# Three small moves in the token mixers: two parted products, V copies behind the first item, a granule chained later

## The chip, the cores and the metric

The kernel runs on one core of one Trainium2 chip. The metric is device time in microseconds, the median of the runs. A core has TensorE (PE in the profile, with its weight loads as PEld), VectorE (DVE), ScalarE (ACT), GpSimd (POOL) and SyncE (SP, which here only issues DMAs).

## The reference

A trunk of two layers on 512 tokens of width 1024, all in float32. A layer is a half-step SwiGLU FFN, a mixers' stage, and a second half-step FFN:

```python
x = x + 0.5 * swiglu(rms_norm(x, ffn1_norm[l]), ffn1_w_in[l], ffn1_w_out[l])
h = rms_norm(x, mix_norm[l]) @ w_mix_in[l]
(c_x, c_b, c_c, h_q, h_f, h_i, h_g, f_q, f_k, f_v, f_f) = jnp.split(h, split_at, axis=-1)
y = jnp.concatenate([
    short_conv_mixer(c_x, c_b, c_c, conv_w[l]),
    hgrn2_mixer(h_q, h_f, h_i, h_g, lower_bounds[l], hgrn_out_gain[l]),
    fox_mixer(f_q, f_k, f_v, f_f, fox_f_bias[l], fox_q_gain[l], fox_k_gain[l]),
], axis=-1)
x = x + y @ w_mix_out[l]
x = x + 0.5 * swiglu(rms_norm(x, ffn2_norm[l]), ffn2_w_in[l], ffn2_w_out[l])
```

The short convolution has 256 channels and three taps. HGRN2 is a gated linear recurrence with four heads of 64, done in chunks of 64 tokens. FoX is causal attention with eight heads of 64, normalised q and k, and a forget gate that adds the difference of cumulative log gates to the logits. D_FF is 2816.

## The kernel before

**Products in three.** Each float32 operand is parted into a high part (rounded to `fp32r`) and a low part, the rest. A product is then three TensorE products, high by high, high by low and low by high, in `mm3` (L322, L330, L331). With `parted=True` the first of the three, high by high, is issued as two halves over the moving operand's columns, so four instructions instead of three. The FFN asks for that at the first product of three of its blocks (`PARTED`, used in `halved`).

**Granules.** Weights come in granules: `granule` loads two rows of 128 (`kk` = 2, or the one that is left) into a buffer `st` (two of them) by SP, and `parted` makes the two parts in a buffer `hl` (three of them): the high part by ACT (L311), the low part by DVE (L312). With `ahead` true this runs at high priority and in one piece. With `ahead` false it has no priority, comes in `kk` pieces, and each piece is put into a given order behind the last named instruction of ACT and of DVE (`follow`, `self.chain`). `stream_steps` yields after each granule's products. Its argument `calm` makes the first granule (`k == 0`) one with `ahead` false.

**The order of instructions.** The kernel is written in Tile: each engine runs its own instructions in order, but what order that is, Tile's scheduler decides from the order in the code, priorities, and what it takes to be ready. The kernel's `NOSYNC` dependencies fix an order where it wants one.

**The mixers' stage** (`mix`) runs once in each layer. It first projects HGRN2's inputs. Then `hgrn`, a generator, alternates with `dense`, the projections of FoX (`fox_qkv`): at each yield `hgrn` says how many granules of `dense` follow, which are 1, 2, 4, 4, 4, 3, 2, 1, 0, 2. `hgrn` issues bursts of small products (64 rows by 64 columns of the array) for the transposes, states and scores of its chunks, and the dense granules fill the time in which DVE and ACT work on them. A granule of `dense` is 2 rows x 4 token tiles x 3 products of 256 columns, 24 in all.

`fox_qkv` runs for two halves of four heads (`hf` = 0, 1). For each it projects q, k and V, and copies V out of two PSUM banks, with the tokens' scale, as a high part (ACT, L1550) and a low part (DVE, L1551); token tiles 0 and 1 lie in the first bank, 2 and 3 in the second. For `hf` = 1 the second bank is `po`, of which there is only one. V of `hf` = 1 is first read in the second run of the attention.

The attention (`fox_attend`) works through 16 items in a run, a head and a tile of 128 queries each. An item has scores (L1602, L1603) issued three items ahead, a softmax (L1607, L274, L1611, L1613 or L1615), four transposes at most into a bank `pt` (L1666; two such banks), their copies PH (ACT, L1668) and PL (DVE, L1669), and, once for two items, the product with V (L1625) into the bank `po`. At a head's first item `fox_prep` also transposes q and k of the head after next into a `pt` bank (L1565), from which KA (ACT, L1570) and QA (DVE, L1571) are made.

`beside` interleaves the attention with dense work: the first run with the convolution's projections (`conv`), the second with five of the eight rows of the output projection (`most`). When `n` is 3 in the first run, `finish` issues HGRN2's end (L1481 to L1490). Last, the stage does the other three rows (`rows(5, ...)`) in two halves of 512 columns, `dg` = 0 and 1; the first of them is `calm`.

Of the kernel before, what the change touches and what calls it, by code (L numbers as in the profile page):

```python
# [1 line left out]

# [39 lines left out]

SKEW_HELD, SKEW_MOVING = 16, 48
PARTED = (10, 16)
EPS = 1e-6
CH = 64
NCH = T // CH
HD = 64
# [109 lines left out]
class Trunk:  # L158
# [8 lines left out]
    def __init__(self, ctx, tc):  # L167
        self.tc = tc
        self.nc = tc.nc
        nc = self.nc  # L170
        self.const = ctx.enter_context(tc.tile_pool(name="const", bufs=1))
        self.res = ctx.enter_context(tc.tile_pool(name="res", bufs=1))
        self.wp = ctx.enter_context(tc.tile_pool(name="wp", bufs=1))
        self.ps = ctx.enter_context(
            tc.tile_pool(name="ps", bufs=1, space=bass.MemoryType.PSUM)
        )
        self.ident = self.const.tile([P, P], F32, tag="ident", name="ident")
        make_identity(nc, self.ident)
        self.ones_mean = self.const.tile([P, P], F32R, tag="ones_mean", name="ones_mean")
        nc.vector.memset(self.ones_mean.bitcast(F32), 1.0 / D)  # L180
        self.epsc = self.const.tile([P, 1], F32, tag="epsc", name="epsc")
        nc.vector.memset(self.epsc, EPS)
        self.xT = self.res.tile([P, KD, T], F32, tag="xT", name="xT")

        self.xh, self.xl = [None] * KD, [None] * KD
        self.uid = 0
        self.ntog = 0
        self.tab, self.tab_users, self.loaded = None, [], None
        self.chain = {}
        self.entry, self.between = {}, {}  # L190
# [127 lines left out]
    def mm3(self, acc, ah, al, bh, bl, first, last, parted=False, keep=False, lows=False):  # L318
        nc = self.nc
        n = bh.shape[-1]  # L320
        for c in (slice(0, n // 2), slice(n // 2, n)) if parted else (slice(0, n),):
            i = nc.tensor.matmul(  # L322
                acc[:, c], ah, bh[:, c], start=first and c.start == 0, stop=False,
                skip_group_check=True,
            )
            if keep:
                self.follow("p", i)
        rest = [(ah, bl), (al, bh)]
        (a, b), (c, d) = rest[::-1] if lows else rest
        nc.tensor.matmul(acc, a, b, start=False, stop=False, skip_group_check=True)  # L330
        i = nc.tensor.matmul(acc, c, d, start=False, stop=last, skip_group_check=True)  # L331
        if keep:
            self.follow("p", i)
# [690 lines left out]
    def mix(self, l, w, w_out, conv_w, out_gain, q_gain, k_gain, f_bias, next_gain):  # L1024
# [3 lines left out]
        with tc.tile_pool(name=self.n("mix"), bufs=1) as mp:  # L1028
# [98 lines left out]
                zf, v[:, :, 256:264], fb.unsqueeze(1).to_broadcast([P, 4, NH])  # L1127
            )
            half = [{}, {}]

            def projections():
                for hf in range(2):
# [5 lines left out]
            for part, n in enumerate(hgrn):  # L1138
                if n is None:
                    break  # L1140
                if n == 0:
                    left.close()
                    ap1 = left.enter_context(
                        tc.tile_pool(name=self.n("at"), bufs=1, reuse_waits="tile")
                    )
                    for tag in ("PH", "PL"):
                        ap1.tile([P, 4, 2, P], F32R, tag=tag, name=self.n(tag), bufs=2)
                    self.qb = pair(ap1, "QB", F32R)
                    for t in self.qb:
                        nc.gpsimd.memset(t[64:66, :].bitcast(F32), 1.0)  # L1150
                    ops = {h: self.fox_prep(ap1, h, half[0][0], qkg, "sc") for h in range(2)}
                if part < 2:
                    next(decay, None)
                for _ in range(n):
                    next(dense, None)
            attend = self.fox_attend(ap1, 0, half, qkg, ops)
# [30 lines left out]
            def beside(attend, dense, first=0, then=()):  # L1187
                for _ in range(first):
                    next(dense, None)
                for n, _ in enumerate(attend, first):  # L1190
                    if n == 3 and then:
                        then()
                    if n >= 2:
                        next(dense, None)
                for _ in dense:
                    pass
# [4 lines left out]
            def rows(k0, a, n):  # L1201
                return lambda k, kk: [
                    w_out[order[k0 + k] * P : (order[k0 + k] + kk) * P, a : a + n]
                ]
# [19 lines left out]
            self.ntog = 0  # L1224
            for dg in range(2):
                banks = self.next4()
                self.stream(
                    [(bk, c, None) for bk, c in zip(banks, TOK)],
                    rows(5, 512 * dg, 512), act(5), 3, calm=dg == 0,
                )  # L1230
                for i in range(4):
                    j = 4 * dg + i
                    add(j, banks[i])
                    self.norm_part(j, ap2)
# [286 lines left out]
    def fox_qkv(self, mp, hf, tokens, half):  # L1521
        nc = self.nc
        qk = mp.tile([P, 4, 4, 2, HD], F32, tag="qk", name=self.n("qk"), bufs=2)
        for w, a in enumerate((F_Q, F_K)):
            banks = yield from tokens(a + 256 * hf, ("mm", "mm" if w == hf else "po"))
            s16 = lambda tag: mp.tile([P, 4, 4], F32, tag=tag, name=self.n(tag), bufs=2)
            m, r, t = s16("fm"), s16("fr"), s16("ft")
            bc = lambda c: c.unsqueeze(2).to_broadcast([P, 4, 4])
            two = lambda bi: slice(2 * bi, 2 * bi + 2)
            src = [x.rearrange("p (i h d) -> p i h d", i=2, h=4) for x in banks]  # L1530
            for bi in range(2):
                out = qk[:, two(bi), :, w, :]
                nc.scalar.activation(out, src[bi], AF.Square)
                nc.vector.reduce_sum(m[:, two(bi)], out, axis=AX.X)
            nc.vector.tensor_mul(m, m, bc(self.inv2))
            self.act(r, m, AF.Ln, bias=self.epsc)
            self.act(r, r, AF.Exp, scale=-0.5)
            self.rsqrt(r, m, r, t)
            nc.vector.tensor_mul(r, r, bc(self.invc))
            for bi in range(2):  # L1540
                out = qk[:, two(bi), :, w, :]
                nc.vector.tensor_mul(
                    out, src[bi], r[:, two(bi)].unsqueeze(3).to_broadcast([P, 2, 4, HD])
                )
        V = mp.tile([P, 4, 4, 2, HD], F32R, tag="V", name=self.n("V"), bufs=2)
        for bi, bank in enumerate((yield from tokens(F_V + 256 * hf, ("mm", "po" if hf else "mm")))):
            for i in (2 * bi, 2 * bi + 1):
                src = bank[:, 256 * (i % 2) : 256 * (i % 2) + 256].rearrange("p (h d) -> p h d", d=HD)
                sc = self.invc[:, i : i + 1]
                nc.scalar.activation(V[:, i, :, 0, :], src, AF.Copy, scale=sc)  # L1550
                nc.vector.scalar_tensor_tensor(  # L1551
                    out=V[:, i, :, 1, :], in0=src, scalar=sc, in1=V[:, i, :, 0, :],
                    op0=ALU.mult, op1=ALU.subtract,
                )
        half[hf] = qk, V

    def fox_prep(self, pool, h, qk, g, tag="pt", second=None):
# [35 lines left out]
    def fox_attend(self, pool, hf, half, g, ops):  # L1593
# [55 lines left out]
        for n, (h, i) in enumerate(items):  # L1649
            yield  # L1650
            if n + LOOK < len(items):
                h2, i2 = items[n + LOOK]
                pb[h2, i2] = scores(ops[h2], i2)
            if i == 0 and h + 2 < NH:
                ops[h + 2] = self.fox_prep(
                    pool, h + 2, half[(h + 2) // 4][0], g, second=nc.gpsimd
                )
            if i % 2 == 0:
                PH, PL = (
                    pool.tile([P, 4, 2, P], F32R, tag=t_, name=self.n(t_), bufs=2)  # L1660
                    for t_ in ("PH", "PL")
                )
            tb = self.bank("pt")
            p = pb.pop((h, i))
            for j in range(i + 1):
                nc.tensor.transpose(tb[:, j * P : (j + 1) * P], p[:, j * P : (j + 1) * P], self.ident)  # L1666
            t3 = tb.rearrange("p (j t) -> p j t", j=4)[:, : i + 1, :]
            nc.scalar.copy(PH[:, : i + 1, i % 2, :], t3)  # L1668
            nc.vector.tensor_sub(PL[:, : i + 1, i % 2, :], t3, PH[:, : i + 1, i % 2, :])  # L1669
            if len(late) and n >= late[0][0] + LAG:  # L1670
                values(*late.pop(0)[1:])
            if i % 2:
                late.append((n, h, i, PH, PL))
        for a in late:
            values(*a[1:])

# [211 lines left out]
```

## Time and profile before

| | us |
|---|---|
| median of three runs | 1805.09 |
| lowest and highest | 1804.33, 1806.71 |
| the profiled execution | 1806.13 |
| its span | 1804.4 |
| busy: PE, DVE, ACT, POOL | 1796.0, 1442.3, 992.8, 176.9 |

The span runs from the first to the last instruction of the program; the profiled execution's own time has some 1.7 us more around it. Matmul records overlap, since each one lasts to the modelled end of its pipeline: the pace of PE is read from one start to the next, not from the durations. The mixers' stage stands at about 340 to 575 us in the first layer and 1230 to 1465 in the second. A row of the timeline gives start, length, engine, line, operation, what is written and read, the shape, the count, and in brackets the idle time before it with what ended it. A row of the chain gives start, length, and what ran.

### The profile page before, as it was taken

How to read it: one execution, taken by the hardware profiler on the slowest of the kernel's cores; microseconds unless marked ns; L12 is line 12 of the kernel's file. 1: busy time of each engine (PE TensorE's matmuls, PEld its weight loads, DVE VectorE, ACT ScalarE, POOL GpSimd, SP SyncE). 2: the span in 40 equal slices, each digit the busy share in tenths (PEclk: the TensorE clock that was granted, in tenths of full speed). 3: DMA queues.
4: the chain of work that ended last, by engine and by line, in shares of the span. 5: the costliest groups of instructions: out<-in, count | busy, mean ns of one | idle time of the engine just before them, and what ended most of it. 6: DMA issues, size and time to landing. Idle time of an engine off the chain costs nothing.

```text
span 1804.4 us, 34742 instructions
## 1 busy us (share of the span) xinstructions
PE 1796.0 (100%) x14267; PEld 1683.9 (93%) x14267; DVE 1442.3 (80%) x2020; ACT 992.8 (55%) x1427; POOL 176.9 (10%) x184
## 2 busy tenths in 40 slices
PE   9999999999999999999999999999999999999999
PEld 7899999899888899999889999998998888999997
DVE  8889887676887898879679887876868778888893
ACT  5455555454776464556445555555547755555551
POOL 0011120100000001112001111201000000020210
PEclk9999999999999999999999999999999999999999
DMA  6658784333433767868266787923234346687762
GB/s 199 186 130 191 183 173 98 76 83 84 105 98 102 220 139 161 196 161 172 82 197 139 171 181 191 174 65 83 78 81 112 92 140 186 164 159 192 157 136 94
DMA packets 244638, 254.09 MB, mean 141 GB/s; under 512 B 18904, under 2 KB 228576, under 8 KB 244480
## 3 DMA queue, kind: packets, MB, share of 16 engines
q1 hardware_dynamic: 189424, 182.38, 33.7%
q0 software_dynamic: 54752, 69.23, 23.8%
q8 instruction: 112, 1.84, 0.4%
q14 instruction: 46, 0.38, 0.1%
q10 hardware_dynamic: 304, 0.27, 0.0%
HBM read 223.98 MB, written 2.10 MB: 125 GB/s over the span
## 4 chain that ended last, share of the span: by engine, by line
PE 93%; DVE 2%; ACT 2%; DMA 1%; issue 1%; SPq 0%; ACTq 0%; DVEq 0%
PE mm L322 13%; PE mm L331 13%; PE mm L330 13%; PE sc L330 6%; PE sc L322 6%; PE sc L331 6%; PE pt L322 6%; PE pt L330 6%; PE pt L331 6%; PE po L331 3%; PE po L322 3%; PE po L330 3%; PE po L1625 1%; PE pt L1666 1%; DMA st<-in_ffn_w_in_dram 1%
## 5 line engine op out<-in xcount | busy, mean ns | idle before, releaser
L804 ACT CAST hl<-w 128x1024 fp32r<-128x1024 f32 x322 | 336.8, 1050 | 310.7 <-PE mm L331 85.4
L806 DVE TENSOR_TENSOR hl<-w,hl 128x1024 fp32r<-128x1024 f32 x322 | 392.4, 1222 | 80.4 <-ACT hl L804 80.1
L312 DVE TENSOR_TENSOR hl<-st,hl 128x512 fp32r<-128x512 f32 (+3 forms) x194 | 162.5, 838 | 116.4 <-ACT hl L311 115.4
L311 ACT CAST hl<-st 128x512 fp32r<-128x512 f32 (+3 forms) x194 | 142.8, 737 | 171.7 <-PE po L331 64.6
L322 PE MATMUL mm<-xc,hl 128*128 128x256 f32 (+1 forms) x733 | 201.2, 276 | 0.0
L330 PE MATMUL mm<-xc,hl 128*128 128x256 f32 x728 | 201.2, 276 | 0.0
L331 PE MATMUL mm<-xc,hl 128*128 128x256 f32 x728 | 201.0, 276 | 0.0
L322 PE MATMUL sc<-xc,hl 128*128 128x256 f32 (+1 forms) x532 | 146.0, 276 | 0.0
L330 PE MATMUL sc<-xc,hl 128*128 128x256 f32 x528 | 146.0, 276 | 0.0
L331 PE MATMUL sc<-xc,hl 128*128 128x256 f32 x528 | 145.8, 276 | 0.0
L322 PEld LDWEIGHTS mm<-xc,hl 128*128 128x128 f32 x733 | 137.4, 188 | 0.2
L330 PEld LDWEIGHTS mm<-xc,hl 128*128 128x128 f32 x728 | 136.7, 188 | 0.0
L331 PEld LDWEIGHTS mm<-xc,hl 128*128 128x128 f32 x728 | 136.7, 188 | 0.0
L322 PE MATMUL pt<-xc,hl 128*128 128x256 f32 (+1 forms) x482 | 132.6, 276 | 0.0
L330 PE MATMUL pt<-xc,hl 128*128 128x256 f32 x480 | 132.6, 276 | 0.0
L331 PE MATMUL pt<-xc,hl 128*128 128x256 f32 x480 | 132.5, 276 | 0.0
L322 PE MATMUL mm<-x,hl 128*128 128x512 f32 x272 | 107.6, 396 | 0.0
L331 PE MATMUL mm<-x,hl 128*128 128x512 f32 x272 | 106.2, 390 | 0.0
L330 PE MATMUL mm<-x,hl 128*128 128x512 f32 x272 | 106.1, 390 | 0.0
L322 PEld LDWEIGHTS sc<-xc,hl 128*128 128x128 f32 x532 | 99.7, 188 | 0.2
L330 PEld LDWEIGHTS sc<-xc,hl 128*128 128x128 f32 x528 | 99.1, 188 | 0.0
L331 PEld LDWEIGHTS sc<-xc,hl 128*128 128x128 f32 x528 | 99.1, 188 | 0.0
(512 smaller groups left out, 5583.1 us busy)
## 6 DMA issues: line engine op xcount, KB each, us to landing
w<-in_ffn_w_in_dram SPq DMA_DIRECT2D x140, 512.0 KB, 5.5
w<-in_ffn_w_out_dram SPq DMA_DIRECT2D x64, 512.0 KB, 4.5
w<-in_ffn_w_out_dram POOLq DMA_DIRECT2D x56, 512.0 KB, 8.4
st<-in_w_mix_in_dram SPq DMA_DIRECT2D x88, 256.0 KB, 2.7
st<-in_ffn_w_in_dram SPq DMA_DIRECT2D x70, 256.0 KB, 3.2
w<-in_ffn_w_in_dram POOLq DMA_DIRECT2D x35, 512.0 KB, 8.1
w<-S POOLq DMA_DIRECT2D x35, 512.0 KB, 4.8
st<-in_ffn_w_out_dram SPq DMA_DIRECT2D x24, 512.0 KB, 5.5
```

What stands on the lines that cost most here:

```text
L311: a = nc.scalar.copy(hi, src[:, c : c + w])
L312: b = nc.vector.tensor_sub(lo, src[:, c : c + w], hi)
L322: i = nc.tensor.matmul(acc[:, c], ah, bh[:, c], start=first and c.start == 0, stop=False, skip_group_check=True,)
L330: nc.tensor.matmul(acc, a, b, start=False, stop=False, skip_group_check=True)
L331: i = nc.tensor.matmul(acc, c, d, start=False, stop=last, skip_group_check=True)
L804: A(nc.scalar.copy(hi, src))
L806: return lambda: V(nc.vector.tensor_sub(lo, src, hi))
L1625: nc.tensor.matmul(self.ob[:, t0 + u * P : t0 + 2 * P], V[:, j, h % 4].rearrange("p a d -> p (a d)"), part[:, j, u:, :].rearrange("p i t - ...
L1666: nc.tensor.transpose(tb[:, j * P : (j + 1) * P], p[:, j * P : (j + 1) * P], self.ident)
```

## The change

Three things, all in the mixers' stage.

- `PAIRS = (1, 5)`: after the yields 1 and 5 of `hgrn` (counted from 0) a counter `self.pair` is set to 2, and `mm3` parts the product at which it comes to 0. This is the second product of the next dense granule, twice in each layer.
- For `hf` = 1 the copies of V's second bank (token tiles 2 and 3) are put on a list, `self.later`, and issued in `beside` when `n` is 1, which is after the first item of the first attention run.
- The first granule of `dg` = 1 becomes `calm` as well, and before it the chain of ACT and DVE is set to `self.turned`: the copies PH and PL of the last head's item with `i == 2` in the second attention run.

```diff
+PAIRS = (1, 5)
...
     def mm3(self, acc, ah, al, bh, bl, first, last, parted=False, keep=False, lows=False):
         nc = self.nc
         n = bh.shape[-1]
+        if self.pair:
+            self.pair -= 1
+            parted |= self.pair == 0
         for c in (slice(0, n // 2), slice(n // 2, n)) if parted else (slice(0, n),):
...
                 if part < 2:
                     next(decay, None)
+                if part in PAIRS:
+                    self.pair = 2
                 for _ in range(n):
                     next(dense, None)
...
                 for n, _ in enumerate(attend, first):
+                    if n == 1:
+                        for copy in self.later:
+                            copy()
+                        self.later = []
                     if n == 3 and then:
                         then()
...
             for dg in range(2):
                 banks = self.next4()
+                if dg:
+                    self.chain["a"], self.chain["v"] = self.turned
                 self.stream(
                     [(bk, c, None) for bk, c in zip(banks, TOK)],
-                    rows(5, 512 * dg, 512), act(5), 3, calm=dg == 0,
+                    rows(5, 512 * dg, 512), act(5), 3, calm=True,
                 )
...
-        for bi, bank in enumerate((yield from tokens(F_V + 256 * hf, ("mm", "po" if hf else "mm")))):
-            for i in (2 * bi, 2 * bi + 1):
-                src = bank[:, 256 * (i % 2) : 256 * (i % 2) + 256].rearrange("p (h d) -> p h d", d=HD)
-                sc = self.invc[:, i : i + 1]
-                nc.scalar.activation(V[:, i, :, 0, :], src, AF.Copy, scale=sc)
-                nc.vector.scalar_tensor_tensor(
-                    out=V[:, i, :, 1, :], in0=src, scalar=sc, in1=V[:, i, :, 0, :],
-                    op0=ALU.mult, op1=ALU.subtract,
-                )
+
+        def copy(i, bank):
+            src = bank[:, 256 * (i % 2) : 256 * (i % 2) + 256].rearrange("p (h d) -> p h d", d=HD)
+            sc = self.invc[:, i : i + 1]
+            nc.scalar.activation(V[:, i, :, 0, :], src, AF.Copy, scale=sc)
+            nc.vector.scalar_tensor_tensor(
+                out=V[:, i, :, 1, :], in0=src, scalar=sc, in1=V[:, i, :, 0, :],
+                op0=ALU.mult, op1=ALU.subtract,
+            )
+
+        banks = yield from tokens(F_V + 256 * hf, ("mm", "po" if hf else "mm"))
+        for i in range(4):
+            if hf and i > 1:
+                self.later.append(partial(copy, i, banks[1]))
+            else:
+                copy(i, banks[i // 2])
...
-            nc.scalar.copy(PH[:, : i + 1, i % 2, :], t3)
-            nc.vector.tensor_sub(PL[:, : i + 1, i % 2, :], t3, PH[:, : i + 1, i % 2, :])
+            a = nc.scalar.copy(PH[:, : i + 1, i % 2, :], t3)
+            b = nc.vector.tensor_sub(PL[:, : i + 1, i % 2, :], t3, PH[:, : i + 1, i % 2, :])
+            if i == 2:
+                turned = a.ins.name, b.ins.name
...
+        self.turned = turned
```

More of the change, by code (lines that the diff above doesn't have):

```diff
@@ L1 @@
 from contextlib import ExitStack
+from functools import partial
 import concourse.bass as bass
@@ L170, in __init__ @@
         nc = self.nc
+        self.pair = 0
         self.const = ctx.enter_context(tc.tile_pool(name="const", bufs=1))
@@ L1190, in beside @@
                 for n, _ in enumerate(attend, first):
+                    if n == 1:
+                        for copy in self.later:
+                            copy()
+                        self.later = []
                     if n == 3 and then:
```

## The prediction

> **What bounds the kernel now.** I read the page first, then PE's waits, then the chain that ended last over the mixers' stage of the first layer, then the timelines of PE, DVE and ACT at the three places that the diff touches. The page:
>
> ```profile
> span 1804.4 us, 34742 instructions
> PE 1796.0 (100%) x14267; PEld 1683.9 (93%) x14267; DVE 1442.3 (80%) x2020; ACT 992.8 (55%) x1427; POOL 176.9 (10%) x184
> ```
>
> TensorE is busy nearly throughout, so the time changes only by what PE waits, or by the pace of its products. The list of PE's waits has these two rows in the mixers, one event in each layer:
>
> ```profile
> PE pt L1666 <- DVE QA L1571: 1.3, 2, 0.7
> PE po L1625 <- ACT PH L1668: 1.0, 2, 0.5
> ```
>
> "Busy" hides a third loss, the pace. In HGRN2's stage PE alternates between bursts of small products (L1510, L1349, L1330, L1388, L1449) and granules of dense ones: 24 products of 256 columns each (two rows, four token tiles, three products), in numbers of 1, 2, 4, 4, 4, 3, 2, 1 after the yields 0 to 7 of `hgrn`. The chain shows the bursts, with start and length, in the first layer:
>
> ```profile
> 388.55 1.32 PE sc L1510 x8
> 395.58 1.08 PE sc L1349 x62
> 396.65 0.90 PE pt L1330 x63
> 409.05 1.97 PE pt L1330 x128
> 422.12 2.00 PE sc L1330 x128
> 435.22 1.06 PE pt L1330 x64
> 436.28 1.95 PE sc L1388 x54
> 446.90 1.06 PE pt L1330 x64
> 453.82 1.09 PE sc L1449 x64
> ```
>
> From the end of one burst to the next, the dense stretches last 5.71 us (389.87 to 395.58, 48 products), 11.50 (397.55 to 409.05, 96), 11.10 (411.02 to 422.12, 96), 11.10 (424.12 to 435.22, 96), 8.67 (438.23 to 446.90, 72) and 5.86 (447.96 to 453.82, 48). The same 96 products take 11.50 us once and 11.10 twice. The stretches of 11.50 and 8.67 differ by 2.83 us and 24 products, 117.9 ns each, which I call the long pace; what is left of 11.50, 0.18 us, is the way in, and with it the stretches of 11.10 run at (11.10 - 0.18) / 96 = 113.8 ns, the short pace. They lie 4.2 ns apart (0.40 us in 96). The pace changes at bursts. At the long pace are the stretches after yields 1, 2, 5, 6 and, by its place between them and the next change, the 24 products after 7: 48 + 96 + 72 + 48 + 24 = 288 products, 288 x 4.2 ns = 1.2 us in each layer.
>
> **Two parted products per layer.** The counter parts the second dense product after yields 1 and 5, at the start of the two series of long-paced stretches. Each of the four in the program adds one 128-column product and one weight load, with no wait and no DMA. The trace has such partings already, in the FFN (L322, `PARTED`), out of a stream at the short pace:
>
> ```profile
> 121.46 0.33 PE L322 MATMUL mm<-xc,hl 128*128 128x128 f32 x2
> ...
> 122.27 0.28 PE L322 MATMUL mm<-xc,hl 128*128 128x256 f32 x1
> ```
>
> Six products' worth lies between them, 0.81 us; at 113.8 ns they take 0.68. A parting costs 0.13 us, 0.52 for four. What it does to a stream at the long pace no row shows; the one above goes in and comes out at the short pace. The gain is bounded by 2 x 1.2 = 2.4 us (both series turn to the short pace and keep it through the small bursts, in both layers). It is (46 + 70) x 4.2 ns = 0.5 us a layer if a burst sets the pace anew. It lies below nothing if a parting hands the long pace to the stretches after yields 3 and 4, which have the short one now and would lose 192 x 4.2 ns = 0.8 us a layer. I take the whole gain: over three of the five changes from a stretch to the next the pace is kept, and the series themselves (1 and 2 long, 3 and 4 short, 5 to 7 long) look like something carried over. Term: 0.52 - 2.4 = -1.9 us; ends -1.9 and +2.1.
>
> The Trainium skill, "TensorE: Matmul & The Clock Gate", section "Back-to-back issue gap", gives one gap for a width when the clock is full, N / 2.4 + 2.5 ns, which is an estimated 109 ns for 256 columns. Neither pace of this trace agrees, and a second pace isn't foreseen; by that rule the parting only adds its cost, the sum would be 2.4 us higher, and the first rival below is that case.
>
> **V's second bank.** Now the copies of V out of the bank `po` (two of L1550 on ACT, two of L1551 on DVE) stand in front of what the next transposes need. PE, DVE and ACT, first layer:
>
> ```profile
> 475.27 0.39 PE L330 MATMUL mm<-x,hl 128*128 128x512 f32 x1
> 475.50 0.39 PE L331 MATMUL mm<-x,hl 128*128 128x512 f32 x1
> 476.53 0.41 PE L1666 MATMUL pt<-ident,P 128*128 128x128 f32 x2 [0.65 <-DVE QA L1571]
> 478.74 0.28 PE L1625 MATMUL po<-PH,V 128*128 128x256 f32 x1
> ```
> ```profile
> 473.18 0.48 DVE L1551 SCALAR_TENSOR_TENSOR V<-po,invc,V 128x256 fp32r<-128x256 f32 x1
> 474.63 0.48 DVE L1551 SCALAR_TENSOR_TENSOR V<-po,invc,V 128x256 fp32r<-128x256 f32 x1
> 475.03 0.68 DVE L1607 CUSTOM_DVE_ANT_0 P<-sc,zm 128x512 f32<-128x512 f32 x1
> 475.64 0.75 DVE L1571 SCALAR_TENSOR_TENSOR QA<-pt,qkg,KA 128x512 fp32r<-128x512 f32 x1
> 476.74 0.67 DVE L1481 TENSOR_SCALAR T<-T 128x1024 f32<-128x1024 f32 x1
> 478.56 0.87 DVE L1669 TENSOR_TENSOR PL<-pt,PH 128x256 fp32r<-128x256 f32 x2
> 479.35 1.21 DVE L1482 TENSOR_TENSOR T<-T,T 128x1024 f32<-128x1024 f32 x1
> 480.60 1.23 DVE L1483 TENSOR_TENSOR T<-T,T 128x1024 f32<-128x1024 f32 x1
> ```
> ```profile
> 472.31 0.47 ACT L1550 ACTIVATE V<-po,invc 128x256 fp32r<-128x256 f32 x1
> 473.55 0.69 ACT L1570 ACTIVATE KA<-pt,qkg 128x512 fp32r<-128x512 f32 x1
> 474.12 0.48 ACT L1550 ACTIVATE V<-po,invc 128x256 fp32r<-128x256 f32 x1
> 475.82 0.72 ACT L274 ACTIVATE P<-P,nm 128x512 f32<-128x512 f32 x1 [1.06 <-DVE nm L1607]
> ```
>
> 512-column products follow one another by 0.23 us, so L1666 was due at 475.73 and came at 476.53: 0.80 us lost. It needs the bank that QA (L1571) reads. The second `po` copy holds DVE for 0.40 us (474.63 to 475.03), and the first, of the same shape and 0.48 us long, for as much. Behind them QA would end at 475.59 instead of 476.39, and PE, 0.14 us later as now, would go on at 475.73. KA on ACT, its other condition, comes earlier by the first copy as well. So the wait goes nearly whole. The two ACT copies fall into the 1.06 us that ACT is idle before 475.82. The two DVE copies, 0.8 us, come behind QA, where DVE's rows stand nearly end to end: behind them are queued the next attention items and HGRN2's end. What is late next is PL of item 1 (478.56), for which the products at 478.74 onward wait; its cover is L1481 (476.74, 0.67 us), work of HGRN2's end that nobody needs soon and that can stand back. Without that cover 0.8 us of the gain comes back as a wait there. The `po` bank must be free for L1625 as well: the copies have some 2 us for it. I take 0.75 us a layer, near the row of the wait: -1.5 us; ends -1.6 and, if the copies come too late (below), well over nothing.
>
> **A granule chained later.** On dg = 1 the high and low copies of the first granule lose their priority, become two pieces each, and are chained behind the attention's copies of the last head's item 2. Now:
>
> ```profile
> 563.07 0.40 PE L322 MATMUL sc<-fyh,hl 128*128 128x512 f32 x1
> 563.98 0.39 PE L1625 MATMUL po<-PH,V 128*128 128x256 f32 x1 [0.52 <-ACT PH L1668]
> 570.65 0.39 PE L322 MATMUL mm<-fyh,hl 128*128 128x512 f32 x1
> ```
> ```profile
> 562.49 1.05 ACT L311 CAST hl<-st 128x1024 fp32r<-128x1024 f32 x1
> 563.56 0.76 ACT L1668 CAST PH<-pt 128x256 fp32r<-128x256 f32 x2
> 574.56 1.04 ACT L311 CAST hl<-st 128x1024 fp32r<-128x1024 f32 x1
> 564.71 0.88 DVE L1669 TENSOR_TENSOR PL<-pt,PH 128x256 fp32r<-128x256 f32 x2
> 564.82 8.56 SPq L294 DMA_DIRECT2D st<-in_ffn_w_in_dram  x4
> ```
>
> L1625 was due at 563.30 and came at 563.98: 0.68 us, for a granule that PE first reads at 570.65. With PH first on ACT, it starts at 562.49 instead of 563.56 and is there in time; the granule's pieces come some 0.9 us later and have over 5 us to spare. The granule's own DMA doesn't move; its buffer `st` is released up to 0.5 us later, and SP's next loads, which wait for it at 564.82, with it. The cast that may use them is at 574.56: covered. The split into pieces adds one instruction on each of ACT and DVE, under the idle time there. Next late would be PL of the same item, which moves up too. Term: 0.65 us a layer, -1.3 us; ends -1.4 and 0 (another order brings another wait).
>
> **Sum.** -1.9 - 1.5 - 1.3 = -4.7 us. The profiled execution took 1806.1 us (span 1804.4 and 1.7 around it), so it would take 1801.4. It stands 1.0 above the median, 1805.1; the median of the changed kernel would be 1800.4.
>
> **Rivals.**
> - *The pace stays.* The parting costs 0.5 us and the long pace stays, or only the rest of a parted stretch gets the short one. For it: the pace changes at bursts, and no parting in the trace is seen to shorten it. Against: the stream behind the parting shown has the short pace, whatever the parting cost it. Gain 2.3 to 3.2 us: 1801.9 to 1802.8. Chance 0.22.
> - *The wait moves on.* DVE, with little room from 475 to 482, gives the 0.8 us back at PL of item 1, so that V's move is worth nothing, and the rest holds: 4.7 - 1.5 = 3.2 us, 1801.9; with some of it left up to 1801.2. Chance 0.13.
> - *The bank comes late: slower.* `po` has one buffer, and the first L1625 of the attention writes it. If the moved copies are queued behind L1482 and L1483 (479.35 to 481.8), they end at 482.6, and PE, which would be at L1625 by 478.0, waits 4.7 us a layer: 9.4 - 1.5 - 1.3 - 1.9 = +4.7, 1809.8. Break-even is a wait of 2.35 us a layer, copies that end after 480.3. Against: in the code the copies are issued behind item 0 and ahead of `finish`, so ahead of L1482. Chance 0.10.
> - *Nothing of it shows*: order elsewhere shifts and takes it back, 1803.5 to 1805.5. Chance 0.05.
>
> **Numbers.** The forecast has 0.50, at 1800.4, own range 1799.4 to 1801.4. I take 0.2% (3.6 us) as about what a measurement of this kernel can tell from no change; its edge is 1801.5. Faster by more: 0.48 of the forecast and 0.04 of the second rival, 0.52. Slower by more: the third rival, 0.10. The rest, 0.38, is within. The range leaves out the case that ends slower, and the far ends: 1799.4 to 1804.4.
>
> **What would show it.** In the chain, the stretches of 96 after yield 2 at 11.1 us in both layers, that of 72 at 8.4 or less plus 0.13. In PE's waits, neither row above. On DVE, QA ahead of both `po` copies, and these done before the first L1625. On ACT, PH ahead of the granule's two pieces. Wrong would be: 117.9 ns behind a parting, 11.5 us for the stretches after yields 3 or 4, or a new wait of PE at L1625 or L1666 around 476 to 480.

## The result and the profile after

| | before | after |
|---|---|---|
| median of 22 runs each, us | 1805.09 | 1802.16 |
| lowest and highest | 1803.61, 1806.71 | 1801.31, 1804.14 |
| the profiled execution | 1806.13 | 1803.06 |
| its span | 1804.4 | 1801.3 |

The ratio is 0.9987, 95% interval 0.9981 to 0.9993: the changed kernel is faster by 2.3 us, between 1.3 and 3.4. The time is inside the predicted range, and 1.8 us above the predicted 1800.4. Two of the three terms came, smaller than predicted; the third, V's second bank, came with the other sign.

The page of the changed kernel and all of its list of PE's waits (engine, line, what waited, for what: us in total, times, longest). Lines are shifted: L1666 is now L1688, L1625 is L1647, L1571 is L1593.

```profile
span 1801.3 us, 34752 instructions
PE 1794.1 (100%) x14271; PEld 1682.1 (93%) x14271; DVE 1441.7 (80%) x2022; ACT 992.6 (55%) x1429; POOL 176.8 (10%) x184
```
```profile
PE pt L1688 <- DVE QA L1593: 1.3, 2, 0.6
PE mm L1805 <- DVE z L1792: 1.2, 1, 1.2
PE po L447 <- ACT sh L438: 0.2, 1, 0.2
PE pt L1688 <- DVE rs L1633: 0.2, 1, 0.2
```

The wait of L1625 for PH is gone. The wait for QA, which V's move was to take away, is there as before: 1.3 us, twice, one in each layer.

The chain that ended last, HGRN2's bursts in the first layer (start, length, what ran):

```profile
394.21 1.08 PE sc L1364 x62
395.29 0.89 PE pt L1345 x63
407.28 1.97 PE pt L1345 x128
420.34 2.00 PE sc L1345 x128
433.44 1.06 PE pt L1345 x64
434.50 1.94 PE sc L1403 x54
444.96 1.06 PE pt L1345 x64
```

The three stretches of 96 products last 11.10 (396.18 to 407.28), 11.09 and 11.10 us, where the first had 11.50; that of 72 lasts 8.52 (436.44 to 444.96), where it had 8.67. The pace has turned, where it was forecast to. But behind the next burst it has turned the other way. PE's timeline, before and then after, from the first dense product behind the transposes that follow yield 9 to HGRN2's sums of squares:

```profile
458.57 0.37 PE L322 MATMUL mm<-hl,x 128*128 128x256 f32 x1
464.11 1.08 PE L1466 MATMUL pt<-T,ones_blk 128*128 128x512 f32 x4
```
```profile
456.33 0.36 PE L328 MATMUL mm<-hl,x 128*128 128x256 f32 x1
462.07 1.10 PE L1481 MATMUL pt<-T,ones_blk 128*128 128x512 f32 x4
```

The same work took 5.54 us and now takes 5.74. Those products had the short pace and have the long one.

**Three stages.** To price the parts I cut each mixers' stage in PE's timeline at three marks. Stage 1 runs from the first dense product behind the forget gate's burst (L1510 before) to the first scores behind the sums of squares (L1466 before); it holds the partings. Stage 2 goes on to the scores of 512 columns of the attention's second head; it holds V's move. Stage 3 goes on to the first parted product of the second FFN; it holds the chained granule. Times are in us, first layer / second layer; the medians are of 11 runs each, except before and after (22 here), and e6 and e13 (one run). The kernel before had a median of 1804.2 to 1804.4 in the runs beside the experiments.

| kernel | median | stage 1 | stage 2 | stage 3 | sum of both |
|---|---|---|---|---|---|
| before | 1805.09 | 75.31 / 75.31 | 19.13 / 18.98 | 141.41 / 141.33 | 471.47 |
| after | 1802.16 | 74.59 / 74.62 | 19.43 / 19.17 | 140.94 / 140.95 | 469.70 |
| after_again | 1802.54 | 74.59 / 74.59 | 19.39 / 18.95 | 140.92 / 140.95 | 469.39 |
| e1, partings alone | 1802.94 | 74.59 / 74.58 | 18.95 / 18.99 | 141.41 / 141.45 | 469.97 |
| e2, V's move alone | 1804.34 | 75.32 / 75.31 | 19.26 / 19.23 | 141.44 / 141.39 | 471.95 |
| e3, chain alone | 1803.01 | 75.31 / 74.69 | 19.11 / 19.02 | 140.89 / 140.94 | 469.96 |
| e4, partings and chain | 1801.94 | 74.59 / 74.59 | 18.97 / 18.93 | 140.88 / 140.87 | 468.83 |
| e5, a third parting | 1802.96 | 74.50 / 74.50 | 19.05 / 19.06 | 140.92 / 140.93 | 468.96 |
| e6, parting at the short pace | 1801.31 | 74.72 / 74.71 | 19.12 / 18.83 | 140.91 / 140.92 | 469.21 |
| e13, late partings | 1801.26 | 74.91 / 74.91 | 19.29 / 18.83 | 140.83 / 140.88 | 469.65 |
| e10, V held | 1801.12 | 74.59 / 74.59 | 18.84 / 18.73 | 140.35 / 140.34 | 467.44 |
| e16, V held otherwise | 1802.19 | 74.59 / 74.58 | 19.20 / 19.00 | 141.03 / 140.96 | 469.36 |
| e15, second run earlier | 1800.46 | 74.62 / 74.62 | 19.19 / 18.90 | 140.41 / 140.33 | 468.07 |
| e17, e16 and e15 | 1801.55 | 74.59 / 74.59 | 19.34 / 18.93 | 140.52 / 140.51 | 468.48 |

Stages 1 and 3 repeat within about 0.1 us, but for stage 1 of e3's second layer (below). Stage 2, in the eight kernels with V's copies where they were, lies between 18.83 and 19.29. The time ahead of the first stage repeats much worse: the forget gate's burst starts at 388.55 in the profile of before and at 387.26 in that of after, but the changed kernel profiled again has it at 386.43. So the 1.3 us which the first two profiles differ by ahead of the mixers is a difference of executions; the mixers hold 1.8 of the 3.1 us between them, and 2.1 in the second profile of after.

### The profile page after: what moved, and what is told of

It reads as the page before. It is cut to its first block, busy times and chain, and to the rows that moved or that the text cites. A ratio compares the mean times of both kernels' runs of the same rounds, so it can differ in the third digit from the quotient of the medians.

```text
span 1801.3 us, 34752 instructions
## 1 busy us (share of the span) xinstructions
PE 1794.1 (100%) x14271; PEld 1682.1 (93%) x14271; DVE 1441.7 (80%) x2022; ACT 992.6 (55%) x1429; POOL 176.8 (10%) x184
## 4 chain that ended last, share of the span: by engine, by line
PE 95%; DVE 2%; ACT 2%; DMA 1%; issue 1%; SPq 0%; ACTq 0%; DVEq 0%
PE mm L328 14%; PE mm L337 14%; PE mm L336 14%; PE sc L328 6%; PE sc L336 6%; PE sc L337 6%; PE pt L328 6%; PE pt L337 6%; PE pt L336 6%; PE po L336 4%; PE po L328 4%; PE po L337 3%; PE po L1647 1%; PE pt L1688 1%; DMA st<-in_w_mix_in_dram 1%
## 5 line engine op out<-in xcount | busy, mean ns | idle before, releaser
L315 DVE TENSOR_TENSOR hl<-st,hl 128x512 fp32r<-128x512 f32 (+3 forms) x196 | 162.7, 831 | 115.6 <-ACT hl L314 114.5
L314 ACT CAST hl<-st 128x512 fp32r<-128x512 f32 (+3 forms) x196 | 143.1, 732 | 174.2 <-PE po L337 67.1
```

The costliest lines, as they stand in the source:

```text
L314: a = nc.scalar.copy(hi, src[:, c : c + w])
L315: b = nc.vector.tensor_sub(lo, src[:, c : c + w], hi)
```

## The experiments

My theory behind the result: the pace is carried from a stretch to the next, and the partings turn it; V's move costs, since the scheduler made another order of it; the chain does what was said, less what it costs PE to go from dense products to products with V and back.

**e1: the partings alone.** The kernel before with `PAIRS = (1, 5)` and the counter in `mm3`.

> Only the two parted products per layer, on top of the kernel before. Theory A, the pace is carried over bursts: the stretches of 96 products after yield 2 last 11.1 us as in the changed kernel, the stretch of 72 some 8.5, and the granules behind the transposes that follow yield 9 turn long (0.2 us a layer lost); net 0.7 us a layer, 1.4 in all, 1803.7 us where the kernel before has 1805.1. Theory B, the gain in the pace only holds together with the other moves or is a matter of the run: stretches of 11.5 us again, and with the cost of four partings, 0.13 us each, 1805.6. A third, that the 1.3 us which the changed kernel's profile gained ahead of the first mixers' stage belong to the partings, would give 1802.4 and the same gain ahead of 340 us; I expect no difference there.

Measured 1802.94 beside 1804.44, ratio 0.999 (0.9981 to 1.0). Stage 1 falls by 0.72 and 0.73 us, as in the changed kernel, and stage 3 stays. Theory A, with the long pace behind the last transposes in it.

**e2: V's move alone.** The kernel before with the list `self.later`.

> Only V's second bank behind the first item, on top of the kernel before. Theory A, the order of the products decides: one of the two copies on VectorE still stands ahead of QA and item 1's transposes are put two products earlier, so the wait for QA stays at 0.6 to 0.7 us in each layer, and the move costs 0.2 to 0.3 us a layer: 1805.5 us where the kernel before has 1805.1, a difference of +0.4 to +0.6. Theory B, my prediction's term, 0.75 us a layer gained: 1803.6, and no wait for QA at item 1's transposes. Theory C, no price at all: 1805.1.

Measured 1804.34 beside 1804.44, ratio 0.9999 (0.999 to 1.0007). The time alone can't tell the theories apart by much; the trace can. It still has both waits, and stage 2 is longer by 0.13 and 0.25 us. From its list of PE's waits:

```profile
PE pt L1686 <- DVE QA L1591: 1.3, 2, 0.6
PE po L1645 <- ACT PH L1688: 1.0, 2, 0.5
```

**e3: the chain alone.** The kernel before with `self.turned` and `calm=True`.

> Only the granule chained later, on top of the kernel before. Theory A: the wait of the product with V for PH goes, and what is left of the 0.68 us is a tenth for each switch between products with V and dense ones; 0.45 to 0.5 us a layer, 1.0 in all, 1804.1 us where the kernel before has 1805.1. Theory B, my prediction's term: 0.65 us a layer, 1803.8. Theory C, the wait goes but comes back at another place: within 0.3 us of the kernel before.

Measured 1803.01 beside 1804.44, ratio 0.9992 (0.9983 to 1.0001). The wait for PH is gone, and stage 3 is shorter by 0.52 and 0.39 us. The two parts of this change, `calm` and the chain behind `self.turned`, were not tried apart. The median gained 0.5 us more than that, and the profile shows where it may lie. The second layer's bursts in the chain, of before and then of e3, which has no parting:

```profile
1287.45 0.89 PE pt L1330 x63
1299.84 1.97 PE pt L1330 x128
```
```profile
1285.01 0.90 PE pt L1345 x63
1297.00 1.97 PE pt L1345 x128
```

The stretch of 96 lasts 11.50 us in the one and 11.09 in the other. In e3 the stretches after yields 1 and 2 of this layer had the short pace by themselves, 0.62 us of stage 1. Without a parting the pace of these stretches isn't given by the kernel's code of that stage alone. What turned it in e3 stays open.

**e4: partings and chain, V's copies as they were.** In the changed kernel:

```diff
-            if hf and i > 1:
+            if False:
```

> The whole change without the move of V's second bank. Theory A, the move of V costs 0.2 to 0.3 us a layer: this kernel is 0.5 us faster than the changed one, 1802.7 us where the changed one has 1803.2 and the kernel before 1805.1 (with 1.4 from the pace and 1.0 from the chain). Theory B, the move of V brought some of the gain: slower than the changed kernel by up to 1.5 us. The parts add up: its gain should be that of the partings alone plus that of the chain alone, to 0.3 us.

Measured 1801.94 beside 1804.44, ratio 0.9988 (0.9979 to 0.9997). By the stages it is 0.6 to 0.9 us faster than the changed kernel, most of it in stage 2. The parts add up: 0.72 + 0.72 in stage 1 and 0.53 + 0.46 in stage 3.

**e13: the partings later in the stretch.** In e4:

```diff
-                    self.pair = 2
+                    self.pair = 14
```

> The change without the move of V's second bank, with the partings at the fourteenth dense product by three instead of the second (after 39 matmuls of the granules instead of 3). Theory A, the parting itself ends the long pace: 117.9 ns from start to start for the 39 products ahead of it and 113.4 behind it, after yield 1 and after yield 5, and the stretches behind stay short; each of the four lasts 36 x 4.4 ns = 0.16 us longer than with the early parting. Theory B, the shift in time or in the order of the program ends it: the short pace from the first product of the stretch. Theory C, the pace is chosen when a stretch begins, so that a late parting does nothing for its own stretch: 117.9 ns to the end.

One run, 1801.26. Stage 1 is 0.32 us longer than in e4 in both layers, which is the expected 0.16 at each of the four partings. PE's timeline after yield 1, around the parting:

```profile
387.08 0.28 PE L328 MATMUL mm<-hl,x 128*128 128x256 f32 x1
...
391.32 0.33 PE L328 MATMUL mm<-hl,x 128*128 128x128 f32 x2
391.49 0.33 PE L336 MATMUL mm<-hl,x 128*128 128x256 f32 x1
...
391.77 0.28 PE L328 MATMUL mm<-hl,x 128*128 128x256 f32 x1
...
392.34 0.28 PE L337 MATMUL mm<-hl,x 128*128 128x256 f32 x1
```

Ahead of the parting 36 products take 4.24 us (387.08 to 391.32), 117.8 ns each; behind it five take 0.57 us, 114 ns, and the next 87 starts in the stretch that follows have a mean of 113.3. Nothing but the place of the parting differs from e4. That the parting itself ends the long pace is shown. Instructions of one shape run here at 117.8 ns and then, some instructions later, at 113.3.

**e6: a further parting, in a stretch at the short pace.** In e4 `PAIRS = (1, 3, 5)`.

> The change without the move of V's second bank, with a further parted product after yield 3, in a stretch that is at the short pace already. Theory A, a parting brings the short pace whatever was before: the stretch after yield 3 lasts 11.10 + 0.13 = 11.23 us, the others are as they were. Theory B, the parting shifts the pace to the other one: 11.10 + 0.13 + 0.40 = 11.6 us, and 11.5 in the stretch after yield 4.

One run, 1801.31. The chain around the stretch after yield 3:

```profile
405.60 1.97 PE pt L1345 x128
418.79 2.00 PE sc L1345 x128
```

It lasts 11.22 us (407.57 to 418.79) instead of 11.10, and the next one 11.10. A parting costs 0.12 to 0.13 us and leaves the short pace short; it isn't a switch between the two. The end of +2.1 us that the prediction kept for the partings is excluded here.

**e5: a third parting, behind the transposes that turn the pace long.** In e4 `PAIRS = (1, 5, 9)`.

> The change without the move of V's second bank, and a third parted product after yield 9, behind the transposes that leave the next 70 products or so at the long pace. Theory A, a parting always brings the short pace: the stretch from those transposes to the next sum, 5.74 us in the kernel with two partings, takes 5.6, and with the products behind it a layer gains 70 x 4.2 ns - 0.13 = 0.17 us: 0.3 us faster than the kernel with two partings, which had 1801.9. Theory B, here the pace belongs to the burst and a parting does nothing: 5.87 us, and 0.3 us slower.

The parting again brings the short pace, a mean of 113.3 ns behind it where there was 117.8. Stage 1 gains 0.09 us, not 0.17, and stage 2 is longer by as much, which is within its spread: 234.47 and 234.49 for the layers, against 234.44 and 234.39 in e4. The median, 1802.96 (ratio 0.9992, 0.9983 to 1.0001), is not better than that of e4, whose interval overlaps and which ran on another chip. So the 0.2 us a layer that the changed kernel loses there is not to be had back in this way.

**e10: V's move in the order that the prediction had in mind.** In the changed kernel, beside names for item 0's PH and PL (`self.opened`) and for the last dense product (`self.product`), `NOSYNC` dependencies for the copies, for the first of HGRN2's end on DVE (the `tensor_scalar`, `i`) and for item 1's transposes. In the first attention run a granule also comes ahead of item 1 instead of item 2:

```diff
-                            copy()
+                            copy(after=self.opened)
...
-                    if n >= 2:
+                    if n == 1 or n > 2 or n == 2 and not first:
                         next(dense, None)
...
+        self.tc.add_manual_dep(i.ins, self.opened[1], NOSYNC, reason="given order")
...
+                if n == 1 and hf == 0 and j == 0:
+                    self.tc.add_manual_dep(tr.ins, self.product, NOSYNC, reason="given order")
```

> The whole change, with V's move as the prediction meant it: the order is held so that both copies of the second bank stand behind item 0's PH and PL on ScalarE and VectorE, HGRN2's end behind item 0's PL, and item 1's transposes behind twelve dense products as before. Theory A, only the scheduler's order spoiled V's term: no wait for QA at item 1's transposes, and 0.5 to 0.75 us a layer faster than the kernel without the move (1801.9), so 1800.4 to 1800.9. Theory B, VectorE has no room and gives it back at PL of item 1 or at the second buffer `po`: a new wait of PE of some 0.7 us in each layer between 474 and 480, and 1801.5 to 1802.5.

Measured 1801.12 beside 1804.40, ratio 0.9981 (0.9972 to 0.999). The gain looks like theory A and isn't. Stage 2 is 0.13 and 0.20 us shorter than in e4; stage 3 is 0.53 shorter, and that is an edit I had not meant: the condition on `n` also puts the dense granules of the second attention run one item earlier. What V's move did is in the waits, and in PE's and DVE's timelines:

```profile
PE po L1651 <- DVE rs L1637: 1.0, 2, 0.5
```
```profile
475.75 0.40 PE L328 MATMUL mm<-x,hl 128*128 128x512 f32 x1
476.62 0.36 PE L1651 MATMUL po<-PH,V 128*128 128x256 f32 x1 [0.47 <-DVE rs L1637]
```
```profile
474.25 1.22 DVE L1499 TENSOR_TENSOR T<-T,T 128x1024 f32<-128x1024 f32 x1
475.39 0.69 DVE L315 TENSOR_TENSOR hl<-st,hl 128x512 fp32r<-128x512 f32 x1
475.99 0.48 DVE L1568 SCALAR_TENSOR_TENSOR V<-po,invc,V 128x256 fp32r<-128x256 f32 x1
```

No wait for QA is left. In its place the first product with V, which writes `po`, waits 0.64 us for the last copy out of `po`: that one ends at 476.47, and PE goes on at 476.62. (The row names `rs`, the next instruction on DVE; by time it is the copy.) This is the mechanism of the prediction's third rival, at a seventh of its price.

**e16: HGRN2's end out of the way.** In e10, the dependency of HGRN2's end on item 1's PL instead of item 0's, and the second run as in the changed kernel.

> The whole change with the order held in the first attention run alone: both copies of V's second bank behind item 0's PH and PL, item 1's transposes behind twelve dense products, and HGRN2's end behind item 1's PL and no longer between the two copies. In the kernel that held it behind item 0, the wait for QA went and one of 0.64 us at the product with V came, since a product of HGRN2's end (1.2 us) stood ahead of the second copy. Theory A, with it out of the way V's move has the worth of the prediction's term: neither wait, 0.7 us a layer faster than the kernel without the move (1801.9), so 1800.4. Theory B, VectorE is short by 0.8 us there whatever the order: another wait of 0.5 us or more between 474 and 486, and at most 0.2 us a layer gained, 1801.5.

Measured 1802.19 beside 1804.24, ratio 0.9986 (0.9977 to 0.9995). PE's waits, and PE, ACT and DVE:

```profile
PE po L1651 <- DVE rs L1637: 1.4, 2, 0.7
```
```profile
474.25 0.39 PE L336 MATMUL mm<-x,hl 128*128 128x512 f32 x1
475.33 0.35 PE L1651 MATMUL po<-PH,V 128*128 128x256 f32 x1 [0.69 <-DVE rs L1637]
```
```profile
473.46 0.60 ACT L314 CAST hl<-st 128x512 fp32r<-128x512 f32 x1
473.97 0.47 ACT L1567 ACTIVATE V<-po,invc 128x256 fp32r<-128x256 f32 x1
```
```profile
474.10 0.69 DVE L315 TENSOR_TENSOR hl<-st,hl 128x512 fp32r<-128x512 f32 x1 [0.71 <-ACT hl L314]
474.70 0.48 DVE L1568 SCALAR_TENSOR_TENSOR V<-po,invc,V 128x256 fp32r<-128x256 f32 x1
```

The wait at `po` grew to 0.85 us, and stage 2 is no shorter than without V's move. So the time is nearer to theory B, but not for its reason: DVE isn't short of room, it stands idle for 0.71 us ahead of 474.10. Now the copy stands behind a dense granule's parting on both engines: DVE's low part (L315) waits for ACT's high part (L314), and the copy of V behind it in the queue waits with it. Copies ahead of that granule were not tried; whether V's move can bring the 0.75 us in that order stays open.

**e15: the second run's granules earlier, without V's move.** In e4:

```diff
-                    if n >= 2:
+                    if n >= 1 + first:
```

> The change without the move of V's second bank, and in the second attention run the dense granules one item earlier (the kernel that held V's order did this unmeant, and its trace gained there 0.53 us in each layer behind 518 us). Theory A, that gain is the earlier granules' alone, dense products where PE waited 0.28 us each, three times, for P and for PH at the turn of the runs: 0.5 us a layer faster than the kernel without it (1801.9), so 1800.9, and no change ahead of 514 us. Theory B, it came with V's move (freer ScalarE and VectorE later on): no gain, 1801.9.

Measured 1800.46 beside 1804.24, ratio 0.9978 (0.997 to 0.9987), the fastest of all; stage 3 is 0.47 and 0.54 us shorter than in e4. Theory A. PE's timeline of e4 shows what was there to gain, where the second run begins:

```profile
520.91 0.27 PE L1647 MATMUL po<-PL,V 128*128 128x128 f32 x1
521.25 0.33 PE L1688 MATMUL pt<-ident,P 128*128 128x128 f32 x1
521.36 0.30 PE L1624 MATMUL sc<-KA,QA 128*128 128x128 f32 x1
521.49 0.29 PE L1625 MATMUL sc<-KB,QB 66*128 66x128 f32 x1
521.85 0.41 PE L1688 MATMUL pt<-ident,P 128*128 128x128 f32 x2
```

Items stand here almost without dense products between them, and PE stops twice for some 0.3 us. In e15 a dense product lies between the two (520.85), and the second gap is gone; the rest of the gain lies further on in stage 3. The median's gain over e4, 1.5 us, is more than the stages' 0.8; the two were not run side by side.

**e17: e16 and e15 together.** In e16 the condition on `n` of e10.

> Both of the last: V's order held with HGRN2's end behind item 1's PL, and the second run's granules one item earlier. If the two gains are apart from one another, 0.7 and 0.53 us a layer, it is 2.4 us faster than the kernel without V's move: 1799.5. If V's gain doesn't come, 1800.7.

Measured 1801.55, ratio 0.9986 (0.9977 to 0.9994), not faster than e15. Stage 3 has most of the gain of the earlier granules, and stage 2 has nothing.

**The changed kernel again.**

> The changed kernel again, beside these, for the price of V's move as it was made. By the traces' marks it costs 0.3 and 0.2 us in the two layers over the pace, and the start of the attention in the kernel without it gains 0.17 more: 0.4 to 0.7 us slower than that one, 1802.4; 2.0 us slower than the kernel with V's order held. If V's move cost nothing, 1801.9. Its profile should have the opening, up to the first mixers' stage, at another time than the one before, by up to 1 us, since that is the same program each time.

Measured 1802.54 beside 1804.24, ratio 0.9989 (0.998 to 0.9998). The opening came 0.8 us earlier than in its first profile. Stage 2 is 0.4 us longer than in e4 in the first layer and the same in the second. The medians of the two, 0.6 us apart and from different sets of runs, do not settle V's price; the stages do, as worked out below.

## Why the prediction was right and wrong

**The partings: right in mechanism, one stretch left out.** Predicted -1.9 us, shown -1.44 (stage 1, twice 0.72, in e1, e4 and after alike). Over the stretches that the prediction counted the gain is what it summed: up to the transposes behind yield 9 a layer of e1 gains 0.94 us, and the prediction's is 1.2 - 2 x 0.13 = 0.94. The choice of the upper end, that the pace is carried through the small bursts, was right for the bursts ahead of yields 2 to 4, 6 and 7, and the second parting was needed: in e13 the 31 starts behind the states' burst (L1403), ahead of the late parting, have a mean of 117.8 ns again. The wrong step was to end the count at yield 7. The burst of transposes behind yield 9 leaves the short pace where the long one came in (5.54 us in before), and the long one where the short one came in (5.74 us in after): 0.22 us a layer back in stage 1. The rival "the pace stays" is out, and with it the case in which a parting only costs; e6 shows that this cost was well sized, 0.12 to 0.13 us.

The prediction tied that rival to the Trainium skill, "TensorE: Matmul & The Clock Gate", section "Back-to-back issue gap". That section calls the formula N / 2.4 + 2.5 ns the gap of an isolated product, says that in a stream the weight loads set the spacing too, and has no figure for a stream of 256 columns. So the formula was the wrong one to set beside these stretches, which run at 117.8 and 113.3 ns; no term of the sum rests on it.

**V's second bank: wrong.** Predicted -1.5 us. Stage 2 has a mean of 19.10 and 18.94 us over the eight kernels with the copies in their old place, and of 19.36 and 19.12 over after, after_again and e2: +0.26 and +0.18, so +0.44 us in all. What sets the two groups of kernels apart lies behind the 128-column scores that follow item 0's transposes: from there to the end of stage 2 the eight take 11.39 to 11.52 us, these three 11.51 to 11.67, without an overlap within a layer; the means differ by 0.14 in each. The other 0.15 us lies ahead of those scores, where item 0's transposes wait for `rs` in some profiles; e13 and e6, without V's move, have such waits too (0.15 and 0.10 us, after has 0.17), so it isn't shown that V's move brought that part.

The step that failed is "Behind them QA would end at 475.59". It moved two copies of 0.40 us from in front of QA. In the changed kernel one of the two still stands there (PE, DVE and ACT, first layer):

```profile
473.17 0.39 PE L328 MATMUL mm<-x,hl 128*128 128x512 f32 x1
474.20 0.41 PE L1688 MATMUL pt<-ident,P 128*128 128x128 f32 x2 [0.64 <-DVE QA L1593]
```
```profile
471.31 0.48 DVE L1566 SCALAR_TENSOR_TENSOR V<-po,invc,V 128x256 fp32r<-128x256 f32 x1
473.30 0.75 DVE L1593 SCALAR_TENSOR_TENSOR QA<-pt,qkg,KA 128x512 fp32r<-128x512 f32 x1
474.41 0.47 DVE L1566 SCALAR_TENSOR_TENSOR V<-po,invc,V 128x256 fp32r<-128x256 f32 x1
```
```profile
472.39 0.49 ACT L1565 ACTIVATE V<-po,invc 128x256 fp32r<-128x256 f32 x1
```

QA did come earlier: 3.79 us behind the scores of 512 columns ahead of it (469.51), where it was 4.09 (471.55 to 475.64). But the scheduler moved item 1's transposes up too: they follow the tenth dense product behind item 0's scores (471.05 to 473.17), where they followed the twelfth (472.92 to 475.50). So PE arrived two products of 0.23 us earlier and waited 0.80 us as before. I had moved DVE's instructions and taken PE's order as given, in a program where the same change sets both. With the order held, QA did start earlier (3.07 us behind those scores in e10, 3.38 in e16) and the wait for it went, but the first product with V waited 0.64 and 0.85 us for the bank `po`. So the rival "the wait moves on" describes what became of V's move, with the wrong place: it named PL of item 1, and the late one is the copy of V itself. PL of item 1 stands right behind that copy on DVE in both kernels, so it isn't shown that PE would have got through with the copy alone out of the way. "They have some 2 us for it" was the cover that the prediction stated and did not set against the queue that the copies were put in.

**The granule chained later: right, with a tail.** Predicted -1.3 us, shown -1.0 (stage 3: 0.52 in the first layer and 0.47 in the second, means of seven kernels with it and three without). PE, ACT and DVE after:

```profile
560.91 0.40 PE L336 MATMUL sc<-fyl,hl 128*128 128x512 f32 x1
561.25 0.39 PE L1647 MATMUL po<-PH,V 128*128 128x256 f32 x1
561.47 0.40 PE L337 MATMUL sc<-fyh,hl 128*128 128x512 f32 x1
```
```profile
560.82 0.75 ACT L1690 CAST PH<-pt 128x256 fp32r<-128x256 f32 x2
561.46 1.15 ACT L314 CAST hl<-st 128x512 fp32r<-128x512 f32 x2
```

PH stands ahead of the granule's two pieces, as forecast. L1647 starts 0.34 us after the product ahead of it, where 0.23 is the usual distance: 0.1 us of the 0.68 stays. A further 0.1 appears from 561.71 to 561.93, where PE goes from one V product of 256 columns to the next block's.

**The sum.** -1.44 + 0.44 - 1.0 = -2.0 us, or -2.2 with only the 0.28 us that is shown for V's move, and the stages of after and after_again give -1.8 and -2.1. It lies inside the intervals of both comparisons (1.3 to 3.4 and 0.4 to 3.6 us faster). The prediction's -4.7 was too much by 2.7 us, of which V's move is 1.9, the burst behind yield 9 0.5, and the chain 0.3. The median of the first comparison differs by 2.9, so that the time came closer to 1800.4 than the working deserved. The bounds held: the range took in the ends at which V's move is worth nothing.

## What to carry to other kernels

When a wait is to be shortened by moving work out of an engine's queue, look at who else the scheduler will move with it: here PE's order closed the gap, and where that was held, the moved copy met the next one who needed its bank. An equal loop that takes two different times is a loss that no list of waits shows; measure it between marks, and try it out with a parting late in the stretch. Cut the program into stages before reading the whole: stages 1 and 3 of the changed kernel repeat to 0.1 us, while the whole differs by more than 1 us between executions.

## What was not expected of the hardware

TensorE ran the same 256-column products at two steady paces, 117.8 and 113.3 ns from start to start, at a granted clock of 1.0 in both. The short pace outlasted bursts of 64 to 128 small products in the changed kernel, and the long one three such bursts in the kernel before. Two bursts changed it there in both layers: long to short at the 128 transposes between the stretches after yields 2 and 3, short to long at the 118 transposes and states ahead of the stretch after yield 5. A product parted into two halves ended the long pace within a few products wherever one was put into it (after yields 1 and 5, early or late, and after 9) and cost 0.12 to 0.13 us at the short pace. The burst of eight 128-column transposes behind yield 9 gave the opposite pace to the one that came in. What in the engine holds this state no run here shows.
